# The mixing of a hybrid trunk layer: projections in small groups, gates and decays through DRAM, heads as series of steps in an order set by a rule

## The chip, the cores and the metric

The kernel runs on one core of one Trainium2 chip. The metric is the device time of one execution in microseconds (us); lower is better. Three executions of the kernel before took 2176.93, 2179.14 and 2181.32 us, with the median at 2179.14.

## What is computed

One layer of a diffusion trunk over 1024 latent tokens, preceded by 256 context tokens that run through the same weights. The model width is 1024, everything in float32. A layer is a half-step SwiGLU feed-forward network, a token mixing and a second half-step network:

```python
x = x + 0.5 * m_l[2][:, None, :] * swiglu(modulate(rms_norm(x, ...), ...), ffn1_w1[i], ffn1_w3[i], ffn1_w2[i])
ctx = ctx + 0.5 * m_c[2][:, None, :] * swiglu(...)
y_l, y_c = token_mixing(modulate(rms_norm(x, ...), ...), modulate(rms_norm(ctx, ...), ...), w_in[i], ...)
x = x + m_l[5][:, None, :] * y_l
x = x + 0.5 * m_l[8][:, None, :] * swiglu(...)
return rms_norm(x, final_norm_w)
```

The mixing projects the tokens with one weight `w_in` and runs two groups of heads, each forwards and backwards: four heads of retention (keys of 128, chunks of 128 tokens, rotary positions, a fixed decay for each head), and four of gated linear attention (GLA; keys of 64, chunks of 64, a decay for each key and token). The latent scans start from the context's final states.

```python
# retention, one chunk
scores = jnp.einsum('bhid,bhjd->bhij', qc, kc) * decay
o = jnp.einsum('bhij,bhje->bhie', scores, vc) + jnp.einsum('bhid,bhde->bhie', qc * q_dec, s)
s = chunk_dec * s + jnp.einsum('bhjd,bhje->bhde', kc * k_dec, vc)
# GLA gates: log decays from a rank-16 projection
g_f = split_heads(jax.nn.log_sigmoid((p[8] @ w_f + b_f).astype(jnp.float32)), GLA_HEADS) / GLA_TAU
# at the end each head is normalised, scaled, multiplied with a silu gate and projected
return jnp.concatenate([r, gl], axis=-1).astype(dtype) @ w_out
```

## The kernel before

**Number format.** A large product is made of three TensorE products of split numbers: `split` (lines 60 and 61) makes a high part on ScalarE and the rest on VectorE or GpSimd, and `mm3` (lines 65 to 67) issues high x high, low x high and high x low into one accumulator. The small products of the heads (128 x 128) are plain float32, two passes each.

**Stages.** First network, context network and context projections (up to about 916 us), then the mixing of the latent tokens (`lat_phase`), the output projection (`mixed_out`) and the second network. In all but the mixing TensorE runs long rows of large products. The latent tokens go in two groups of 512 (`tg` 0 and 1).

**The mixing.** `lat_phase` (line 1309) runs a list of calls, `SEQ`: projections of a pair of GLA heads, gates, context heads, projections of retention heads, head by head. Projections: `gla_proj_pair` (values and the input `p89T` of the gates with `proj_v`, then queries and keys), `ret_proj` (queries and keys with the rotary turn: a copy with partitions exchanged by SP's queue, lines 1101 to 1108), `gate_proj` (silu gates `sg`). Their results stay in SBUF (`qk`, `vt`, `sg`). `proj_v` copies out four accumulators `psa` (lines 919 and 922); the 32-column copies `p` (922) are transposed (923) into `p89T`. There are four accumulators `psa` for projections, and others, `psb`, for the heads.

**Heads.** `gla_gates` (line 1112) makes the gate tiles of one head and group: a product (1118), the softplus on ScalarE (812 to 816: Abs, a load of a function table where `load` is set, Exp, Ln), a subtraction on VectorE, seven sums on GpSimd (1126) and two Exps (1128, 1129). `gla_mix` makes scores on seven block sizes: copies into `zq` and `zk` (1156 to 1159), a product (1163), a multiplication of A on VectorE (1183) and B on GpSimd (1184); the two largest sizes use small products (1174, 1175). Then come key transposes (1199), state updates (1205, 1212) and output products (1219, 1220). `ret_mix` has key transposes (1252), products for states (1265), scores (1278) and output (1291, 1293), statistics (1297, 1299), a power on GpSimd (`pow_half`, 1072 and 1073) and the normalisation (1305). Both end in `finish` (1054): four transposes on TensorE (1059), a multiplication with norm weight and silu gate (1066), and a store to `mixd` in DRAM by SP's queue. Where the silu gate isn't made yet, retention heads 2 and 3, the tile is kept (1062) and multiplied in `mixed_in` (1351).

**What sets the order.** A scheduler puts every engine's instructions in order from the program order, priorities and its own times. `high_priority(offset=-...)` with `FPRI`, `VPRI`, `RPRI` and `CRP` moves transposes of `finish`, state products, key transposes and context products back; weight loads have an own priority. A queue runs in its order, so an instruction that waits holds up what stands behind it. SP's queue issues loads; GpSimd's issues the stores of the networks (`self.store`, line 351) and none in the mixing.

## Time and profile before

| | before |
|---|---|
| runs, median (lowest to highest) | 2179.14 us (2176.93 to 2181.32) |
| profiled execution: time, span of the trace | 2177.08 us, 2175.3 us |
| TensorE busy | 2115.8 us, 97% |
| VectorE, ScalarE, GpSimd busy | 1533.8, 980.5, 367.3 us |
| mean granted clock of TensorE, of full speed | 0.995 |

The rows below come from one profiled execution, whose time differs a little from its span, since what lies before the first and after the last instruction is not in the span. PE is TensorE, DVE VectorE, ACT ScalarE, POOL GpSimd; L12 is line 12 of the kernel. The time of a matmul record includes its filling of the array, so records overlap and the pitch from start to start is shorter.

### The profile page before, as it was taken

Reading aid. Unit: us, or ns where it says so; the run is one execution under the profiler, and the core shown is the slowest. Engines: PE = TensorE matmul, PEld = TensorE weight load, DVE = VectorE, ACT = ScalarE, POOL = GpSimd, SP = SyncE. Lnnn points to the kernel's source line nnn. Section 1 sums busy time; section 2 is a strip of 40 time slices with the busy share of each in tenths; the row PEclk is TensorE's granted clock in tenths of the full one; section 3 lists DMA queues with packets and bytes.
Section 4 is the critical chain, followed back from the end, with each engine's and each line's share of the span. In section 5 each row is a group of like instructions: output and inputs, shape, how many; then the busy total and the mean of one; then the engine's idle time right before and its main releaser. Section 6 shows DMA issues by size and latency. Waiting matters only on the chain. (4 is left out here: it accounts for less than half of the span.)

```text
span 2175.3 us, 33087 instructions
## 1 busy us (share of the span) xinstructions
PE 2115.8 (97%) x11558; PEld 1805.0 (83%) x11558; DVE 1533.8 (71%) x2747; ACT 980.5 (45%) x1811; POOL 367.3 (17%) x472
## 2 busy tenths in 40 slices
...
GB/s 331 83 232 242 266 221 270 179 241 309 296 196 172 169 184 194 184 144 104 90 65 62 103 60 82 119 92 155 63 129 161 139 155 158 155 221 242 207 242 148
DMA packets 190263, 373.40 MB, mean 172 GB/s; under 512 B 24016, under 2 KB 37264, under 8 KB 190096
## 3 DMA queue, kind: packets, MB, share of 16 engines
...
q14 instruction: 77, 0.63, 0.1%
q10 hardware_dynamic: 432, 0.13, 0.0%
...
## 5 line engine op out<-in xcount | busy, mean ns | idle before, releaser
L60 ACT ACTIVATE whi<-raw 128x512 fp32r<-128x512 f32 (+1 forms) x647 | 398.2, 622 | 667.2 <-PE psa L66 200.0
L61 DVE TENSOR_TENSOR wlo<-raw,whi 128x512 fp32r<-128x512 f32 (+1 forms) x545 | 377.4, 696 | 292.3 <-ACT whi L60 289.0
L67 PE MATMUL psa<-hh,wlo 128*128 128x512 f32 (+1 forms) x1444 | 530.0, 367 | 3.1 <-POOL wlo L61 3.1
L65 PE MATMUL psa<-hh,whi 128*128 128x512 f32 (+1 forms) x1444 | 530.6, 367 | 1.1 <-DVE s L565 0.6
L66 PE MATMUL psa<-hl,whi 128*128 128x512 f32 (+1 forms) x1444 | 529.8, 367 | 0.6 <-DVE hl L61 0.6
L67 PEld LDWEIGHTS psa<-hh,wlo 128*128 128x128 f32 x1444 | 273.3, 189 | 45.3 <-POOL wlo L61 4.1
L65 PEld LDWEIGHTS psa<-hh,whi 128*128 128x128 f32 x1444 | 273.4, 189 | 44.6 <-DVE s L565 1.0
L66 PEld LDWEIGHTS psa<-hl,whi 128*128 128x128 f32 x1444 | 273.5, 189 | 42.1 <-DVE hl L61 1.2
L65 PE MATMUL psb<-hh,whi 128*128 128x512 f32 (+1 forms) x680 | 260.0, 382 | 0.5 <-ACT whi L60 0.5
L67 PE MATMUL psb<-hh,wlo 128*128 128x512 f32 (+1 forms) x680 | 259.9, 382 | 0.6 <-DVE wlo L61 0.6
L66 PE MATMUL psb<-hl,whi 128*128 128x512 f32 (+1 forms) x680 | 259.7, 382 | 0.0
L61 POOL TENSOR_TENSOR wlo<-raw,whi 128x512 fp32r<-128x512 f32 (+1 forms) x102 | 136.7, 1358 | 204.5 <-ACT whi L60 200.5
L351 POOL DMA_DIRECT2D gd<-s x154 | 83.7, 543 | 392.1 <-DVE s L342 300.5
L67 PEld LDWEIGHTS psb<-hh,wlo 128*128 128x128 f32 x680 | 127.9, 188 | 25.7 <-DVE wlo L61 1.3
L65 PEld LDWEIGHTS psb<-hh,whi 128*128 128x128 f32 x680 | 128.0, 188 | 25.5 <-ACT whi L60 1.0
L66 PEld LDWEIGHTS psb<-hl,whi 128*128 128x128 f32 x680 | 127.9, 188 | 24.8
L66 PE MATMUL psa<-wlo,hh 128*128 128x256 f32 (+1 forms) x320 | 93.4, 292 | 1.2 <-DVE wlo L61 1.1
L65 PE MATMUL psa<-whi,hh 128*128 128x256 f32 (+1 forms) x320 | 93.3, 292 | 1.2 <-ACT s L1027 1.2
L67 PE MATMUL psa<-whi,hl 128*128 128x256 f32 (+1 forms) x320 | 92.7, 290 | 0.0
L128 DVE CUSTOM_DVE_ANT_0 junk<-ada,condc,cols 128x1024 bf16<-128x1024 f32 x62 | 79.4, 1281 | 5.7 <-DMA ada<-in_adaT 3.9
L1073 POOL TENSOR_TENSOR nr<-nr,mhalf 128x4 f32<-128x4 f32 (+1 forms) x11 | 10.6, 965 | 412.6 <-DVE nr L1072 403.0
L61 DVE TENSOR_TENSOR hl<-raw,hh 128x512 fp32r<-128x512 f32 x93 | 65.2, 709 | 10.4 <-ACT hh L60 10.3
(404 smaller groups left out, 3884.0 us busy)
## 6 DMA issues: line engine op xcount, KB each, us to landing
...
gd<-s POOLq DMA_DIRECT2D x154, 256.0 KB, 3.0
...
```

Of the source, the lines that this page charges most:

```text
L60: nc.scalar.activation(hi, src, AF.Copy)
L61: (eng or nc.vector).tensor_tensor(out=lo, in0=src, in1=hi.bitcast(F32), op=ALU.subtract)
L65: mm(ps, wa[0], xa[0], start=start, stop=False, skip_group_check=more)
L66: mm(ps, wa[0], xa[1], start=False, stop=False, skip_group_check=more)
L67: mm(ps, wa[1], xa[0], start=False, stop=stop, skip_group_check=more)
L128: nc.vector.tensor_tensor_reduce(out=self.junk, in0=t, in1=self.cs[s], scale=1.0, scalar=self.col("ada_b")[:, j:j + 1], op0=ALU.mult, op1= ...
L351: put = lambda i, t: self.store.dma_start(self.gd[i, f // 2], t)
L1073: nc.gpsimd.tensor_tensor(out=r, in0=r, in1=self.mhalf[:, :n], op=ALU.pow)
```

## The change

The arithmetic and TensorE's 10,746 products stay the same; the mixing is laid out anew.

- Projections become `units`, series of pieces of 6 or 12 products in the order of a list `UNITS`. Each unit copies its accumulators to a tile `pv` and stores it to DRAM by GpSimd's queue (`put`). Value weights are loaded once for both token groups (except those of `gv0`, which also makes the gates' input).
- Gates of all four heads of a group are made in a row (`gate_lane`), those of group 0 after the unit `ga0` and those of group 1 after `gv0`; they go to DRAM. The decays of the retention heads are made once behind the first group's gates and go to DRAM.
- Heads become four `lanes` of steps: context heads, gates, GLA heads, retention heads. A step yields the earliest time at which TensorE should take it, its cost, and the names of units and gates it needs.
- `lat_phase` writes TensorE's whole order: the step of a lane whose time has come, else the next piece of a projection. The times come from sums of VectorE's work (`vec`, times `SLACK` 1.25) and constants. The other engines are still put in order by the scheduler.
- 15 of the 16 head tiles are now multiplied with their silu gate in `mixed_in`, from DRAM, where before it were 4.
- Table loads are asked for in the first gate only. On ScalarE the program has 27 of them before and 5 after. Stores of context states and head tiles move from SP's queue to GpSimd's: 198 DMAs there before, 298 after; on SP's 1260 and 1292.

```diff
+    def finish(self, on, tg, wcol, hb, pool):
         nc = self.nc
         pt = self.psB()
-        with self.tc.high_priority(offset=-FPRI):
-            for c in range(4):
-                nc.tensor.transpose(pt[:, c * P:(c + 1) * P], on[:, c * P:(c + 1) * P], self.ident)
-        if sg is None:
-            t = self.tile(pool, [P, 512], F32, "qk", 8)
-            nc.scalar.activation(t, pt, AF.Copy, scale=wcol)
-            self.late[hb, tg] = t
+        for c in range(4):
+            nc.tensor.transpose(pt[:, c * P:(c + 1) * P], on[:, c * P:(c + 1) * P], self.ident)
+        mx = self.t2(pool)
+        if hb in self.gated:
+            sg = self.tile(pool, [P, 512], F32, "sg", 2)
+            nc.sync.dma_start(sg, self.sgd[hb * P:(hb + 1) * P, tg * 512:(tg + 1) * 512])
+            nc.vector.scalar_tensor_tensor(out=mx, in0=pt, scalar=wcol, in1=sg, op0=ALU.mult, op1=ALU.mult)
         else:
-            mx = self.t2(pool)
-            nc.vector.scalar_tensor_tensor(out=mx, in0=pt, scalar=wcol, in1=sg[tg], op0=ALU.mult, op1=ALU.mult)
-            nc.sync.dma_start(self.mixd[hb * P:(hb + 1) * P, tg * 512:(tg + 1) * 512], mx)
+            self.late.add((hb, tg))
+            nc.scalar.activation(mx, pt, AF.Copy, scale=wcol)
+        self.store.dma_start(self.mixd[hb * P:(hb + 1) * P, tg * 512:(tg + 1) * 512], mx)
...
+    def gate_lane(self, pool):
+        nc = self.nc
         for tg in LATTG:
...
+            yield 0, 0, (("ga0", "gv0")[tg],)
+            for h in range(4):
+                yield self.now, 0.45, ()
+                self.gla_gates(h, tg, pool)
+                self.done[f"G{tg}{h}"] = self.vec(1.4) + 6
+            if tg == 0:
+                for h in range(4):
+                    self.decays(h, pool)
+
+    def decays(self, h, pool):
+        nc = self.nc
+        tab = lambda i: self.tab[:, i * P:(i + 1) * P]
+        dec, u = self.tile(pool, [P, 3, P], F32, "dec", 1), self.t2(pool)[:, :P]
+        lf, lb = self.lg[:, h:h + 1], self.lg[:, 4 + h:5 + h]
+        for o, i, l in ((dec[:, 0, :], 0, lf), (u, 1, lb), (dec[:, 1, :], 2, lf), (dec[:, 2, :], 3, lb)):
+            nc.scalar.activation(o, tab(i), AF.Exp, scale=l)
+        nc.vector.tensor_tensor(out=dec[:, 0, :], in0=dec[:, 0, :], in1=tab(4), op=ALU.mult)
+        nc.vector.tensor_tensor(out=u, in0=u, in1=tab(5), op=ALU.mult)
+        nc.vector.tensor_tensor(out=dec[:, 0, :], in0=dec[:, 0, :], in1=u, op=ALU.add)
+        self.store.dma_start(self.decd[h], dec.rearrange("p i t -> p (i t)"))
+        self.done[f"D{h}"] = self.vec(0.6) + 4
...
-        self.softplus(a, zp, bias, tg in LXG)
+        self.softplus(a, zp, bias, (h, tg) == (0, 0))
...
+        self.store.dma_start(self.ggd[h, tg], g)
+        self.store.dma_start(self.gLd[h, tg][:, :508], L[:, :508])
+
+    def vec(self, us):
+        self.dve = max(self.dve, self.now) + SLACK * us
+        return self.dve
...
+            ons.append((self.vec(1) + 3 - 2 * (tg == 0), on))
+        for tg in LATTG:
+            yield ons[tg][0], 0.9, ()
+            self.finish(ons[tg][1], tg, self.col("ret_norm_w")[:, h:h + 1], h, pool)
...
+    def put(self, pool, ps, dst, fn=AF.Copy, scale=1.0, view=None):
+        t = self.tile(pool, [P, 512], F32, "pv", 4)
+        self.nc.scalar.activation(t, ps, fn, scale=scale)
+        self.store.dma_start(dst, view(t) if view else t)
+
+    def unit(self, pool, w, dst, fn=AF.Copy, scale=1.0):
+        for tg in LATTG:
+            ps = self.psA()
+            for q in range(4):
+                yield 4 * tg + q, q // 2, 6 * 0.227
+                for k in range(2 * q, 2 * q + 2):
+                    self.mm3(ps, self.wslice(w, k), self.h[tg][k], k == 0, k == KD - 1)
+            self.put(pool, ps, dst[:, tg * 512:(tg + 1) * 512], fn, scale)
...
+    def unit_v0(self, pool, w, tg):
+        nc = self.nc
+        ps = [self.psA() for _ in range(4)]
+        for k in range(KD):
+            yield k, k, 12 * 0.133
+            for c in range(4):
+                self.mm3(ps[c][:, :288], [t[:, c * P:(c + 1) * P] for t in self.h[tg][k]], [t[:, :288] for t in w[k]], k == 0, k == KD - 1)
+        pT = self.psB()
+        if tg == 0:
+            self.pt89 = self.tile(pool, [64, 512], F32, "p89T", 1)
+        rs = []
+        for c in range(4):
+            r = self.tile(pool, [P, 32], F32, "p89", 4)
+            nc.scalar.copy(r, ps[c][:, 256:288])
+            rs.append(r)
+        t = [self.tile(pool, [P, 512], F32, "pv", 4) for _ in range(2)]
+        for c in range(4):
+            nc.scalar.copy(t[c // 2][:, c % 2 * 256:c % 2 * 256 + 256], ps[c][:, :256])
+        for c in range(2):
+            r0 = 512 * tg + 256 * c
+            self.store.dma_start(self.gvd[r0:r0 + 256, :256].rearrange("(c p) e -> p c e", p=P), t[c].rearrange("p (c e) -> p c e", c=2))
+        yield KD, None, 0.5
+        for c in range(4):
+            nc.tensor.transpose(pT[:32, c * P:(c + 1) * P], rs[c], self.ident)
+        self.p89T[tg] = self.pt89[32 * tg:32 * tg + 32]
+        nc.scalar.copy(self.p89T[tg], pT[:32])
...
+        self.now, self.dve = 0.0, 0.0
+
+        def step(lane):
+            y = next(lane[0], None)
+            if y is None:
+                lanes.remove(lane)
+            else:
+                lane[1:] = y
+
+        lanes = [[g, 0, 0, ()] for g in lanes]
+        with self.pe_order():
+            for lane in list(lanes):
+                step(lane)
+            piece = next(fill, None)
+            while lanes or piece:
+                ready = [(max([x[1]] + [done[n] + DONE for n in x[3]]), i) for i, x in enumerate(lanes) if all(n in done for n in x[3])]
+                at, i = min(ready) if ready else (1e9, None)
+                if i is not None and (at <= self.now or not piece):
+                    self.now = max(self.now, at) + lanes[i][2]
+                    step(lanes[i])
+                elif piece:
+                    name, work, pe = piece
+                    self.vec(work / SLACK)
+                    self.now += pe
+                    if name:
+                        done[name] = self.now
+                        if name[1] == "g":
+                            self.gated.add(int(name[2]) + 4 * (name[0] == "g"))
+                    piece = next(fill, None)
 
     def mixed_in(self, pool):
         nc = self.nc
...
         zt, i = [f"z{n}{h}" for h in (1, 2, 4, 8, 16) for n in "qk"], 0
         for tg in LATTG:
             for k in KORD:
+                s = (slice(k * P, (k + 1) * P), slice(tg * 512, (tg + 1) * 512))
+                raw = self.tile(pool, [P, 512], F32, zt[i % len(zt)])
+                i += 1
+                nc.sync.dma_start(raw, self.mixd[s])
                 if (k, tg) in self.late:
-                    raw = self.late[k, tg]
-                    nc.vector.tensor_tensor(out=raw, in0=raw, in1=self.late_sg[k][tg], op=ALU.mult)
-                else:
-                    raw = self.tile(pool, [P, 512], F32, zt[i % len(zt)])
-                    i += 1
-                    nc.sync.dma_start(raw, self.mixd[k * P:(k + 1) * P, tg * 512:(tg + 1) * 512])
+                    sg = self.tile(pool, [P, 512], F32, "qk", 4)
+                    nc.sync.dma_start(sg, self.sgd[s])
+                    nc.vector.tensor_tensor(out=raw, in0=raw, in1=sg, op=ALU.mult)
...
-LXC = (0, 1, 2, 3)
-LXG = (0, 1)
+LXC = (0,)
...
-SEQ = ('gla_in(0)', 'gates(0)', 'cr()', 'cg()', 'ret_in(0)', 'gla(0)', 'gates(1)', 'ret(0)', 'gla(1)', 'gates(2)', 'ret(1)', 'gla_in(1)', 'ret_in(1)', 'gla(2)', 'gates(3)', 'ret(2, False)', 'gla(3)', 'ret(3, False)')
+UNITS = ("gv0", "gk0", "gq0", "rk0", "rq0", "rv0", "rk1", "rq1", "gk1", "gq1", "gv1", "gg0", "rg0", "gg1", "rk2", "rq2", "rv1",
+         "rg1", "rk3", "rq3", "gg2", "rg2", "gg3", "rg3")
+WAHEAD, WLIVE = 3, 5
+SLACK = 1.25
+CTXAT = 16
+DONE = 6
```

Instruction orders below are rows of the two programs, in the form line, operation, out<-in, shape.

ScalarE in the start of the mixing, before: `vt` and `p` are the copies of the value projection of the second group, `p89T` the gates' input, L812 to L816 the gates of the first head.

```order
L919 COPY vt_9974<-psa_10145 128x256
L922 COPY p_2325_10300<-psa_10144 128x32
L922 COPY p_2326_10304<-psa_10145 128x32
L60 ACTIVATE whi_10759<-raw_10757 128x512
L926 COPY p89T_10123<-psb_10290 32x512
...
L812 ACTIVATE t_2348_10441<-psb_10442,cols_78 128x512
L814 ACT_TABLE_LOAD
L815 ACTIVATE t_2348_10441<-t_2348_10441 128x512
L812 ACTIVATE t_2352_10464<-psb_10465,cols_78 128x512
L816 ACTIVATE t_2348_10441<-t_2348_10441 128x512
```

After: L818, L1091 and L1092 are Ln and Exps of the gates (`sc` and `L` of heads 2 and 3), L817 their Exp, L1068 the decays, L972 a context copy, L1393 the `p` copies of the second group.

```order
L1091 ACTIVATE sc_10330<-sc_10330 128x512
L818 ACTIVATE t_2345_10345<-t_2345_10345 128x512
L1068 ACTIVATE t_2351_10379<-tab_9877,lgx_9879 128x128
L1068 ACTIVATE t_2353_10389<-tab_9877,lgx_9879 128x128
L1068 ACTIVATE t_2355_10399<-tab_9877,lgx_9879 128x128
L1092 ACTIVATE L_10320<-L_10320 128x508
L1091 ACTIVATE sc_10354<-sc_10354 128x512
L1068 ACTIVATE dec_10378<-tab_9877,lgx_9879 128x128 x3
L972 COPY t_2360_10429<-psb_10426 128x256
L1393 COPY p_2369_10485<-psa_10169 128x32
L1393 COPY p_2370_10487<-psa_10170 128x32
L1393 COPY p_2371_10489<-psa_10171 128x32
```

The `p` copies of the second group stood ahead of all gates and now stand behind the gates of four heads.

TensorE at the end of the first retention head, before: L1291 and L1293 are the head's output products, L1059 the transposes of `finish`, L65 to L67 projection products, of which 13 lie between.

```order
L1291 MATMUL psb_11716<-vt_10722,t_2574_11710 128x128
L1293 MATMUL psb_11716<-S_11646,t_2575_11712 128x128
L1293 MATMUL psb_11716<-S_11646,t_2576_11714 128x128
L65 MATMUL psa_12258<-hh_2071_9185,whi_12240 128x512
L66 MATMUL psa_12258<-hl_2072_9186,whi_12240 128x512
...
L67 MATMUL psa_12294<-hh_2061_9175,wlo_12247 128x512
L65 MATMUL psa_12294<-hh_2063_9177,whi_12246 128x512
L1059 MATMUL psb_11750<-ident_82,t_2581_11745 128x128
L1278 MATMUL psb_11758<-qk_11532,qk_11568 128x128 x4
L1059 MATMUL psb_11750<-ident_82,t_2581_11745 128x128 x3
```

After: L1342 and L1344 are output products, L1033 transposes of `finish` (the first two rows of them of a GLA head, the last of this retention head's group 0), L67 to L69 projections, of which 18 lie between.

```order
L1344 MATMUL psb_11856<-Sr_11541,t2r_11829 128x128
L1033 MATMUL psb_11893<-ident_82,t_2595_11796 128x128 x4
L1033 MATMUL psb_11901<-ident_82,t_2600_11817 128x128 x4
L67 MATMUL psa_11771<-hh_1331_5977,whi_11452 128x512
L68 MATMUL psa_11771<-hl_1332_5978,whi_11452 128x512
...
L68 MATMUL psa_11940<-hl_2068_9182,whi_11470 128x512
L69 MATMUL psa_11940<-hh_2067_9181,wlo_11471 128x512
L1342 MATMUL psb_11965<-vr_11539,t2r_11886 128x128
L1344 MATMUL psb_11965<-Sr_11541,t2r_11882 128x128
...
L1344 MATMUL psb_11965<-Sr_11541,t2r_11882 128x128
L1344 MATMUL psb_11965<-Sr_11541,t2r_11884 128x128
L1033 MATMUL psb_12006<-ident_82,t2r_11888 128x128 x4
```

The transposes of a group now come after the other head's transposes, 18 projection products and the next group's output.

GpSimd at heads' ends, before: L1184 are multiplications of the scores, L1073 the power in a head's end.

```order
L1184 TENSOR_TENSOR B_2823_13356<-B_2823_13356,L_12186 128x8x32
L1184 TENSOR_TENSOR B_2825_13362<-B_2825_13362,L_12209 128x8x32
L1184 TENSOR_TENSOR B_2823_13356<-B_2823_13356,L_12186 128x4x64
L1184 TENSOR_TENSOR B_2825_13362<-B_2825_13362,L_12209 128x4x64
L1073 TENSOR_TENSOR rr_13616<-rr_13616,mhalf_86 128x4
L1073 TENSOR_TENSOR rr_13648<-rr_13648,mhalf_86 128x4
```

After: L1048 is the power, L1145 the multiplication, L1369 and L1042 are stores of projections and head tiles.

```order
L1048 TENSOR_TENSOR rr_12620<-rr_12620,mhalf_86 128x4
L1369 DMA gvd<-pv_12779 128x2x256
L1042 DMA mixd<-t_2740_12740 128x512
L1048 TENSOR_TENSOR rr_12727<-rr_12727,mhalf_86 128x4
L1369 DMA gvd<-pv_12782 128x2x256
L1369 DMA gvd<-pv_12785 128x2x256
L1369 DMA gvd<-pv_12788 128x2x256
L1048 TENSOR_TENSOR rr_12804<-rr_12804,mhalf_86 128x4
```

Stores now stand between these instructions; ten of the 16 powers have one right ahead.

## Rows read from the trace of the kernel before

**Rows 1.** The page: busy time, share of the span and instructions of each engine

```profile
PE 2115.8 (97%) x11558; PEld 1805.0 (83%) x11558; DVE 1533.8 (71%) x2747; ACT 980.5 (45%) x1811; POOL 367.3 (17%) x472
```

**Rows 2.** Stretches: us, busy (x) of PE, PEld, DVE, ACT, POOL; clock; DMA share; GB/s

```profile
916.00:1020.00 104.00, 94.93 (x613) 84.60 (x612) 48.90 (x126) 55.11 (x130) 20.31 (x33) 0.98 0.47 134
1020.00:1440.00 420.00, 399.64 (x2736) 340.36 (x2734) 260.31 (x599) 194.17 (x373) 87.26 (x115) 1.00 0.27 81
1440.00:1462.00 22.00, 20.22 (x99) 16.50 (x100) 11.45 (x28) 7.58 (x12) 1.31 (x1) 1.00 0.32 100
```

**Rows 3.** TensorE's waits, 1020 to 1462: line, waited for, us, times, longest

```profile
PE psb L1059 <- DVE t L1305: 6.1, 5, 2.5
PE psb L1059 <- ACT t L1230: 3.7, 5, 1.0
PE psb L1163 <- ACT zq L1157: 3.2, 4, 1.0
PE psb L1174 <- POOL B L1184: 3.1, 5, 1.1
PE psb L1163 <- DVE zk L1158: 2.0, 3, 1.1
...
```

**Rows 4.** TensorE's waits, 916 to 1020, same view

```profile
PE psb L995 <- DVE t L990: 4.3, 2, 2.5
PE psb L923 <- ACT p L922: 1.4, 1, 1.4
...
```

**Rows 5.** Timeline of TensorE at the end of a lane's run

```profile
1058.08 0.48 PE L66 MATMUL psa<-hl,whi 128*128 128x512 f32 x1
1058.39 0.40 PE L67 MATMUL psa<-hh,wlo 128*128 128x512 f32 x1
1058.63 0.39 PE L65 MATMUL psa<-hh,whi 128*128 128x512 f32 x1
1058.86 0.39 PE L66 MATMUL psa<-hl,whi 128*128 128x512 f32 x1
```

**Rows 6.** Timeline of ScalarE at two gates

```profile
979.66 1.28 ACT L814 ACT_TABLE_LOAD   x1
980.95 0.63 ACT L815 ACTIVATE t<-t 128x512 f32<-128x512 f32 x1
981.49 0.67 ACT L812 ACTIVATE t<-psb,cols 128x512 f32<-128x512 f32 x1
```

**Rows 7.** Timeline of GpSimd at the first gate's sums

```profile
983.69 0.61 POOL L1126 TENSOR_TENSOR L<-sc 128x256 f32<-128x256 f32 x1 [45.11 <-DVE sc L1122]
984.39 2.43 POOL L1126 TENSOR_TENSOR L<-L 128x128 f32<-128x128 f32 x6
```

**Rows 8.** Stores of the FFN issued by GpSimd, line 351

```profile
L351 POOL DMA_DIRECT2D gd<-s x154: 539/539/736, 66.7 to 1955.7; - x154
...
DMA to landing us min/median/max: 2.2/3.0/7.3
```

**Rows 9.** Groups of VectorE by form, 925 to 1475

```profile
L1305 DVE TENSOR_SCALAR t<-psb,bmv,rr 128x128 f32<-128x128 f32 x32 | 10.9, 404 | 7.0 <-POOL rr L1073 7.0
...
L1297 DVE BATCH_NORM_STATS2 bst<-psb 128x6 f32<-128x128 f32 x32 | 7.1, 282 | 4.8 <-PE psb L1293 4.8
...
L1299 DVE BATCH_NORM_AGGREGATE bmv<-bst 128x2 f32<-128x6 f32 x32 | 2.9, 151 | 0.0
...
L1351 DVE TENSOR_TENSOR qk<-qk,sg 128x512 f32<-128x512 f32 x4 | 2.7, 686 | 0.0
...
L1072 DVE TENSOR_SCALAR rr<-bmv 128x4 f32<-128x4 f32 x8 | 1.3, 163 | 0.1
```

**Rows 10.** Groups of GpSimd by form, 925 to 1475

```profile
L1184 POOL TENSOR_TENSOR B<-B,L 128x256 f32<-128x256 f32 x48 | 40.9, 857 | 62.2 <-DVE zk L1158 45.2 <-PE psb L1175 6.4 <-DVE rr L1072 5.0
L1073 POOL TENSOR_TENSOR rr<-rr,mhalf 128x4 f32<-128x4 f32 x16 | 18.1, 1132 | 159.1 <-DVE rr L1072 159.1
```

**Rows 11.** Groups of ScalarE by form, 925 to 1475: busy us, mean ns, idle before

```profile
L1157 ACT COPY zq<-B 64x256 f32<-64x256 f32 x40 | 16.5, 411 | 47.2 <-PE psb L1163 28.6 <-POOL B L1184 14.1 <-POOL B L1155 4.3
```

484 lines of the change are left out of this document (271 added, 213 removed).

## The prediction

> **What bounds the kernel now.** I read the busy table first: TensorE is busy for 2115.8 us, 97% of the span [rows 1]. A change that leaves its matmuls alone can at most win the rest, so the question is where TensorE is not busy in the part that is rewritten, the mixing from 916 to 1462 us. The table by stretches [rows 2] gives that: in the start (916 to 1020: context heads, first gates, first projections) TensorE is busy 94.93 of 104 us, in the middle 399.64 of 420, in the last 22 us 20.22. That is 9.1 + 20.4 + 1.8 = 31.3 us, and the clock hardly enters (0.98 to 1.00). The program order has 10,746 matmuls before and after, of the same shapes; hence everything is in these 31 us and in small costs of switching.
>
> Then I read what ended TensorE's waits. From 1020 on they add up to 21.4 us in nine rows, of which the first five stand in [rows 3]: transposes at a head's end wait for VectorE's normalised tile (6.1) or ScalarE's (3.7), score products for the zq/zk copies (3.2 and 2.0), small block products for GpSimd (3.1). All are short (at most 2.5 us), 28 in number: before gives a chain too little other TensorE work to run beside. In the start, 4.3 of 8.9 us are waits of the context retention for its decayed values and 1.4 for p, the 32-column copies from which the gates' input is transposed [rows 4].
>
> **Part 1, the start: 12.6 us dearer.** After ga0 (gates' input of token group 0) TensorE issues all four heads' gate products at once, and ScalarE works them off in one row: order on ScalarE shows Abs, Exp, Ln and two more Exps for heads 0 to 2, those of head 3 but its last Exp, seven Exps of decays, and only then the p copies L1393 of the second token group. TensorE has, from the first gate product to the transposes L1403 that need these copies, the four gate products in f32 (two passes each), 48 products of 288 columns and two context transposes. By the pitch of about 0.23 us for 512 columns [rows 5], 288 columns take about 0.13, so 6.3 us for the 48, 1.8 for the gates and 0.5 for the transposes: 8.6 us. It can't go past them: the second group holds all four "psa" accumulators, which the next projection needs too.
>
> The chain on the other side, by durations of before: Abs, table load, Exp and Ln of the first head follow at a pitch of about 0.54 with the load at 1.28 [rows 6], some 3.5 us; subtraction on VectorE about 1.5; then GpSimd's seven sums of one gate, from 983.69 to 986.82, 3.1 us [rows 7], and behind them in its queue two stores at 0.54 each [rows 8]. Three gates' sums in a row, the third without its stores: 5.0 + 2 x 4.2 + 3.1 = 16.5. After the last Exp of head 2 come one of head 3, three decays and a context copy at 0.4, then the copies of 32 columns: some 20 us, and up to 23 with the hand-overs. TensorE stands 11.5 to 14.5 us; I take 13.5, nearer the upper end since weight splits stand between. To this come 2 us for the first group's copies and transposes (before 1.4), 2.7 for the second gates and a context transpose behind them, 1.5 for context loads that wait for stores, and 2 for the clock, which shows in the stretch at 0.98 even now: 21.7 us, against 9.1. Net +12.6, range +6 to +16.
>
> ScalarE loses 22 table loads of 1.28 us, 28 us of its time [rows 6]. In this chain one load remains where before each pair of gates had two. The row says that a load costs its 1.28 us and no more: load at 979.66, next Exp at 980.95. The Trainium skill (ScalarE: Activation LUTs, What ACT_TABLE_LOAD costs) adds a drain of about 1.38 us to each switch, 2.66 in all. By that rule ScalarE would get back 58 us instead of 28, and the one load that is left in the start's chain would make the time 2172.0. The trace disagrees, since nothing idles around the load, and I use neither number.
>
> **Part 2, the middle: 19 us cheaper.** The steps are now laid out so that a chain has its time beside it in projection pieces. At the end of a retention head the chain is 4 x 0.282 + 4 x 0.151 + 0.163 + 1.132 + 4 x 0.404 = 4.64 us [rows 9, 10], about 5.1 with hand-overs. Before: 13 products of 512 columns between output and transposes, 3.0 us, and TensorE waits up to 2.5 [rows 3]. After, for head 0: between the output of group 0 and its transposes lie 8 other transposes, 18 products and the output of group 1, 0.9 + 4.1 + 2.7 = 7.7 us; for group 1, 24 products and 8 small ones, 6.8. Both cover 5.1. Score products have 12 to 18 projection products ahead (2.8 to 4.1 us) instead of 6 (1.4), against copies of 0.41 us on two engines [rows 11] and one GpSimd multiplication of 0.857 [rows 10]. Of the 21.4 us of waits, with about a tenth of restart at each of 28, 24 us, I let 5 stay, since the rule counts VectorE's work and not ScalarE's, GpSimd's or the DMAs': -19, bounds -8 (16 stay) and -23 (1 stays).
>
> **Part 3, fewer returns: 3.6 us cheaper.** Where a run of small products ends, the first projection product takes 0.31 instead of 0.23 us to the next [rows 5]. In the order I count 125 such returns before and 80 after: 45 x 0.08 = 3.6 us. Bounds 0 and 5.
>
> **Part 4, traffic and the end: 1.5 us dearer.** q, k, v, gates and decays go to DRAM by about 100 more GpSimd stores, 0.539 us each to issue and 3.0 to land [rows 8]: 54 us of GpSimd, which is busy 109 of the 546 us (the three stretches of [rows 2]), and DMA engines busy 0.27. Hidden but for one place: the last retention head's transposes have 18 products ahead (4.1 us) against 5.1, and its tile then goes to DRAM and back, twice 3.0 us, and is multiplied and split. I count 9.9 us against 10.3 us of output projections that need other tiles first. The 15 late tiles instead of 4 add 11 multiplications of 0.686 on VectorE [rows 9], 7.5 us; VectorE is busy half of that last stretch. Together 1.5, bounds 0 and 6. The value weights loaded once for both groups take 12 splits off ScalarE and VectorE: nobody on the path waits for these in the middle, so nothing.
>
> **Sum** on the profiled execution (2177.08 us): 12.6 - 19 - 3.6 + 1.5 = -8.5, so 2168.6. The median of the runs lies 2.06 us higher: **2170.6 us**, 0.4% faster.
>
> **The rivals.**
> - *The start costs little.* If the copies L1393 come at the early end or GpSimd's sums do not wait for the stores (the second sums could begin 1.1 us sooner per gate), and the middle leaves 1 us: 2170.6 - 6.6 - 4 = 2160. For it: ScalarE's and GpSimd's pieces overlap at before's pitch. Against: the row on ScalarE is fixed, and four gates' sums on one engine alone are 12 us against 8.6 of cover.
> - *Slower: GpSimd's queue.* Ten of the 16 power instructions at heads' ends stand directly behind a store in GpSimd's order, often of a projection that has yet to be evicted, and none did before. A unit of projection takes 24 x 0.23 = 5.5 us; a mean wait of half, 2.8 us, is over the slack of 1.7 (6.8 less 5.1) by 1.1 us, so 11 us; the multiplications L1145 stand behind stores as well, and if the waits of the scores and blocks come back (3.2 + 3.1 + 2.0 = 8.3), the time is 2190. It decides from a mean wait of 1.7 us on. For it: the rule knows nothing of GpSimd. Against: the evictions are of units that the order has before the head's end, and waiting stores were 0.54 us each.
> - *GpSimd's stores are slow beside VectorE.* A store takes 539 ns to issue at the median and 736 at most, and lands after up to 7.3 us [rows 8], beside a busy VectorE. If all landed late: 4.3 us more at the end and 0.2 x 8 in the gates' chain, 2176.5. The Trainium skill (SBUF — State Buffer, the warning on the "DVE blocks DMA" trap) says that such a store cannot write its descriptors while VectorE runs a float32 copy in its two-port mode. The maximum of 736 beside 539 hardly shows it, though no store ran in the mixing of before, where VectorE's copies into zq and zk are.
> - *Nothing gained:* the middle keeps 14 of its waits: about 2179.
>
> **How the numbers follow.** My forecast gets 0.45, the cheap start 0.17, the slower queue 0.22, the slow stores 0.08, nothing gained 0.08. A difference under 0.2% (4.4 us) is about what a measurement of this kernel can't tell from no change, so "same" runs from 2174.8 to 2183.5. The forecast's own spread (start +6 to +16, middle -23 to -8) puts some 0.08 of its 0.45 into same. Faster: 0.37 + 0.17 + 0.01 = 0.55. Same: 0.08 + 0.07 + 0.07 + 0.01 = 0.23. Slower: 0.22. The range is 2152 to 2192: below, the cheap start at no net cost (6 us less than its +6) and the returns at their bound (1.4), 2160 - 7.4 = 2152.6; above, the queue rival at 2190 and part of the end's bound.
>
> **What would show it.** In the start of the changed trace one wait of 10 us or more at L1403 for ScalarE's p, with GpSimd's sums of three gates before it. After about 1020 us TensorE's waits sum to under 10 us, at L1033 under 3. The power instructions start within a microsecond of VectorE's input. If L1403 waits under 5 us, part 1 is wrong; if L1033 or the scores wait for GpSimd by more than before, part 2 is; and if ScalarE's busy time in the mixing does not fall by about 28 us, the table loads were miscounted.

## The result: slower by 0.4%

| | before | after |
|---|---|---|
| median of five runs | 2178.75 us | 2187.05 us |
| lowest to highest | 2176.93 to 2181.32 | 2184.12 to 2192.70 |
| ratio, 95% interval | | 1.0040, 1.0024 to 1.0057 |
| profiled execution, span | 2177.08, 2175.3 us | 2184.12, 2180.9 us |
| mean granted clock | 0.995 | 0.989 |

The changed kernel is 8.3 us slower, where 8.5 us faster was forecast. In the profiled executions the difference is 7.0 us, 5.6 us of it inside the traces' spans.

The first line of the changed kernel's page, busy time by engine:

```profile
PE 2119.4 (97%) x11558; PEld 1817.0 (83%) x11558; DVE 1529.7 (70%) x2735; ACT 948.6 (43%) x1776; POOL 420.5 (19%) x572
```

TensorE is *busy* for 3.6 us more than before [rows 1] with the same products. Some of them ran more slowly, as the clock below shows.

Stretches of the mixing, after (us of the stretch; busy time and count on PE, PEld, DVE, ACT and POOL; clock; DMA share; GB/s):

```profile
916.00:1027.00 111.00, 91.35 (x472) 74.99 (x471) 58.74 (x139) 66.63 (x154) 54.05 (x109) 0.91 0.59 192
1027.00:1440.00 413.00, 398.41 (x2844) 354.16 (x2843) 244.27 (x578) 149.15 (x308) 106.80 (x139) 0.98 0.47 147
```

The start has 111 - 91.35 = 19.65 us without TensorE, the middle 14.6, the end none. Before it was 9.1, 20.4 and 1.8 [rows 2]. Idle time in the mixing has thus grown by 3.0 us only. But the clock is 0.91 in the start and 0.98 in the middle.

TensorE's waits in the start of the changed kernel, and in the rest of the mixing (line, waited for, us, times, longest). L1403 are the transposes of the `p` copies, L950, L956, L970 and L981 steps of context heads, L1153 the scores of a GLA head and L1033 the transposes of `finish`:

```profile
PE psb L1403 <- ACT p L1393: 12.0, 2, 11.5
PE psb L981 <- ACT t L818: 3.9, 1, 3.9
PE psb L950 <- DVE t L946: 1.9, 1, 1.9
...
```

```profile
PE psb L1153 <- DVE zq L1131: 4.5, 1, 4.5
PE psb L1033 <- ACT t L1240: 3.8, 3, 2.9
PE psb L1033 <- DVE t2r L1359: 2.1, 2, 1.5
...
```

The waits of the middle that stood in [rows 3] have become fewer (12 of 14.4 us in all, against 28 of 21.4), but three of those that are left are long: 4.5, 2.9 and 1.5 us. In [rows 4] the longest was 2.5; here one is 11.5.

That one, on TensorE, then on ScalarE, then on GpSimd:

```profile
959.49 0.29 PE L69 MATMUL psa<-whi,hl 128*128 128x288 f32 x1
971.33 1.03 PE L1403 MATMUL psb<-ident,p 128*32 128x128 f32 x4 [11.54 <-ACT p L1393]
```

```profile
950.07 0.69 ACT L814 ACTIVATE t<-psb,cols 128x512 f32<-128x512 f32 x1
950.77 1.28 ACT L816 ACT_TABLE_LOAD   x1
952.07 0.63 ACT L817 ACTIVATE t<-t 128x512 f32<-128x512 f32 x1
...
957.74 0.63 ACT L1092 ACTIVATE L<-L 128x508 f32<-128x508 f32 x1 [1.72 <-POOL L L1089]
...
963.06 0.63 ACT L1092 ACTIVATE L<-L 128x508 f32<-128x508 f32 x1 [1.71 <-POOL L L1089]
...
968.87 0.63 ACT L1092 ACTIVATE L<-L 128x508 f32<-128x508 f32 x1 [1.19 <-POOL L L1089]
...
971.09 0.44 ACT L1393 COPY p<-psa 128x32 f32<-128x32 f32 x4
```

```profile
954.74 0.61 POOL L1089 TENSOR_TENSOR L<-sc 128x256 f32<-128x256 f32 x1 [3.59 <-DVE sc L1085]
955.43 2.27 POOL L1089 TENSOR_TENSOR L<-L 128x128 f32<-128x128 f32 x6
957.83 0.56 POOL L1093 DMA_DIRECT2D ggd<-sc  x1
958.77 0.54 POOL L1094 DMA_DIRECT2D gLd<-L  x1 [0.37 <-ACT L L1092]
959.70 0.98 POOL L1089 TENSOR_TENSOR L<-sc 128x256 f32<-128x256 f32 x1 [0.39 <-DVE sc L1085]
```

TensorE ends its last 288-column product at 959.8 and has its next instruction at 971.3. ScalarE goes through the gates in its fixed order: each Exp of the sums (L1092, at 957.74, 963.06 and 968.87) waits for one gate's sums on GpSimd, whose first instructions are 5.0 us apart (954.74, 959.70), the two stores L1093 and L1094 among them. The `p` copies come at 971.09, 21.0 us after the first gate's Abs at 950.07. That is the chain of the prediction, near its length.

What TensorE had to do beside it was not as counted. The prediction gave the four gate products 1.8 us, eight passes at the pitch of the large products. Before and after:

```profile
977.80 1.13 PE L1118 MATMUL psb<-p89T,wg 32*128 32x512 f32 x4
```

```profile
947.83 3.82 PE L1081 MATMUL psb<-p89T,wg 32*128 32x512 f32 x8
```

Before, the products of a head's two token groups start in pairs, within 0.01 us of each other, and the four passes take 1.1 us. After, with one group at a time, the passes follow each other at 0.43 us, and eight take 3.8. From the first of them, at 947.83, to the transposes are 23.5 us. TensorE works for 12.0 of these, not 8.6 as counted, some of it at the lower clock shown next, and stands for 11.5.

**The clock around it.** The same stretch in pieces:

```profile
946.80:951.60 4.80, 4.80 (x15) 2.06 (x13) 2.14 (x3) 2.52 (x5) 0.57 (x1) 0.97 0.92 332
951.60:954.70 3.10, 3.10 (x14) 3.08 (x14) 1.35 (x2) 3.09 (x6) 0.00 (x0) 0.50 0.40 134
...
959.80:971.30 11.50, 0.00 (x0) 0.00 (x0) 6.54 (x15) 8.26 (x22) 9.22 (x23) 0.72 0.44 154
971.30:974.80 3.50, 3.47 (x11) 2.77 (x12) 0.79 (x4) 2.67 (x10) 3.03 (x9) 0.50 0.56 230
```

From 951.3 on the granted clock was 0.50 (1.2 of 2.4 GHz) for 3.4 us, a half-clock stretch as it is called below, at the end of the four gate products, which use 32 rows; from 964.9 to 975.2 again, first while TensorE stood, then for another 3.8 us in which it worked. There are four more such stretches in the mixing, at 995.6 (6.8 us), 1132.2 (3.4), 1207.3 (3.4) and 1292.6 (6.8). Each of the four begins during a wait or at most 1.5 us behind its end; these waits are 3.9, 1.5, 2.9 and 4.5 us long. Before, there were two, of 3.4 us each, at 999.2 and 1347.3, behind waits of 2.5 and 2.0 us; a third wait of 2.5 us, at 1117.3, had none. The first of them, the wait and the stretch behind it:

```profile
995.20:997.60 2.40, 0.00 (x0) 0.03 (x1) 1.96 (x7) 2.33 (x7) 1.05 (x2) 1.00 0.43 104
998.80:1002.20 3.40, 3.40 (x19) 3.38 (x19) 2.69 (x8) 1.67 (x4) 0.68 (x1) 0.55 0.35 117
```

**The account.** I counted, from TensorE's records and the granted clock of windows of 0.4 us, for each kernel the time from the first 288-column product to a fixed product of the second network (the 2780th from the end of the three-product kind), the idle time in it, and half of the time that TensorE worked at half clock. What is left is work at full clock:

| kernel | stretch | idle | lost by the clock | rest |
|---|---|---|---|---|
| before | 655.9 | 34.2 | 3.4 | 618.3 |
| after | 662.3 | 36.4 | 12.8 | 613.1 |

So the order did make the work itself 5.2 us cheaper; the idle time grew by 2.2 in this longer stretch, and the clock took 9.4 us more. The sum, +6.4, is the difference of the stretches. The rest of the span adds -0.8 us.

### The profile page after: what moved, and what is told of

Read it like the earlier page. It is cut to its first block, busy times and chain, and to the rows that moved or that the text cites. A ratio compares the mean times of both kernels' runs of the same rounds, so it can differ in the third digit from the quotient of the medians.

```text
span 2180.9 us, 33346 instructions
## 1 busy us (share of the span) xinstructions
PE 2119.4 (97%) x11558; PEld 1817.0 (83%) x11558; DVE 1529.7 (70%) x2735; ACT 948.6 (43%) x1776; POOL 420.5 (19%) x572
## 4 chain that ended last, share of the span: by engine, by line
PE 79%; DVE 6%; issue 5%; DMA 4%; POOL 2%; ACT 2%; SPq 0%; POOLq 0%; ACTq 0%; DVEq 0%
PE psa L67 14%; PE psa L69 14%; PE psa L68 14%; PE psb L67 10%; PE psb L69 9%; PE psb L68 9%; PE psa L1421 3%; PE psb L1153 2%; DVE hl L226 1%; POOL L L1089 1%; DVE nt L220 1%; DMA qk<-sgd 1%; DMA raw<-in_w 1%; PE psb L1301 1%; POOL rr L1048 0%
## 5 line engine op out<-in xcount | busy, mean ns | idle before, releaser
L62 ACT ACTIVATE whi<-raw 128x512 fp32r<-128x512 f32 (+1 forms) x635 | 390.7, 622 | 673.2 <-PE psa L68 212.6
L63 DVE TENSOR_TENSOR wlo<-raw,whi 128x512 fp32r<-128x512 f32 (+1 forms) x533 | 368.2, 694 | 251.6 <-ACT whi L62 244.1
L67 PE MATMUL psa<-hh,whi 128*128 128x512 f32 (+1 forms) x1444 | 535.8, 371 | 2.2 <-ACT hh L62 1.1
L69 PE MATMUL psa<-hh,wlo 128*128 128x512 f32 (+1 forms) x1444 | 528.9, 366 | 3.1 <-POOL wlo L63 3.1
L67 PEld LDWEIGHTS psa<-hh,whi 128*128 128x128 f32 x1444 | 275.4, 191 | 47.1 <-ACT hh L62 1.9
L69 PEld LDWEIGHTS psa<-hh,wlo 128*128 128x128 f32 x1444 | 274.2, 190 | 48.0 <-POOL wlo L63 4.1
L67 PE MATMUL psb<-hh,whi 128*128 128x512 f32 (+1 forms) x680 | 259.6, 382 | 0.5 <-ACT whi L62 0.5
L69 PE MATMUL psb<-hh,wlo 128*128 128x512 f32 (+1 forms) x680 | 259.5, 382 | 0.6 <-DVE wlo L63 0.6
L69 PEld LDWEIGHTS psb<-hh,wlo 128*128 128x128 f32 x680 | 127.8, 188 | 25.7 <-DVE wlo L63 1.0
L67 PEld LDWEIGHTS psb<-hh,whi 128*128 128x128 f32 x680 | 127.8, 188 | 25.5 <-ACT whi L62 1.0
L1048 POOL TENSOR_TENSOR nr<-nr,mhalf 128x4 f32<-128x4 f32 (+1 forms) x11 | 10.3, 932 | 423.1 <-DVE nr L1047 413.5
L385 POOL DMA_DIRECT2D sd<-s x22 | 11.9, 541 | 359.3 <-DVE s L384 359.2
L62 ACT ACTIVATE hh<-raw 128x512 fp32r<-128x512 f32 x93 | 57.0, 620 | 12.2 <-DMA raw<-gd 9.8
L352 DVE TENSOR_TENSOR s<-s,s 128x512 f32<-128x512 f32 x88 | 59.0, 685 | 0.4
```

The lines of the kernel that those rows point to most:

```text
L62: nc.scalar.activation(hi, src, AF.Copy)
L63: (eng or nc.vector).tensor_tensor(out=lo, in0=src, in1=hi.bitcast(F32), op=ALU.subtract)
L67: mm(ps, wa[0], xa[0], start=start, stop=False, skip_group_check=more)
L69: mm(ps, wa[1], xa[0], start=False, stop=stop, skip_group_check=more)
L352: sub = lambda o, a, b: nc.vector.tensor_tensor(out=o, in0=a, in1=b, op=ALU.subtract)
```

## Experiments

All but the two probes start from the changed kernel. Times are medians; ratios are against the kernel before, run in turn on the same chip (there 2179.53, 2178.01 and 2176.92 us in the three groups). The changed kernel was not run again beside them, so differences to its 2187.05 us are good to 2 or 3 us. The last column is the account as above, for the profiled execution of each run:

| run | time | ratio, 95% interval | stretch = idle + clock + rest |
|---|---|---|---|
| e8_prio | 2186.88 | 1.0037 (1.0023 to 1.0051) | 668.0 = 38.7 + 15.6 + 613.7 |
| e5_spread | 2179.76 | 1.0001 (0.9989 to 1.0012) | 652.9 = 30.6 + 7.4 + 614.9 |
| e2_filler | 2188.06 | 1.0048 (1.0030 to 1.0065) | 668.1 = 27.7 + 16.7 + 623.7 |
| e3_rope2 | 2190.22 | 1.0046 (1.0031 to 1.0062) | 666.5 = 37.4 + 17.2 + 611.9 |
| f1_spread_ctx | 2183.37 | 1.0023 (1.0013 to 1.0032) | 659.2 = 34.9 + 11.0 + 613.3 |
| f3_room | 2173.85 | 0.9979 (0.9969 to 0.9989) | 650.0 = 27.4 + 10.8 + 611.8 |
| e4_loads_back | 2193.55 | 1.0075 (1.0058 to 1.0092) | 670.3 = 45.4 + 11.3 + 613.6 |
| e7_sp_stores | 2179.79 | 1.0013 (1.0002 to 1.0023) | 657.8 = 34.9 + 9.5 + 613.4 |
| b_pause0 | 2186.87 | 1.0050 (1.0033 to 1.0066) | 664.8 = 38.5 + 8.1 + 618.2 |
| b_pause16 | 2197.67 | 1.0095 (1.0078 to 1.0111) | 676.4 = 49.3 + 8.9 + 618.2 |
| g1_room_sp | 2165.29 | 0.9941 (0.9923 to 0.9958) | 641.5 = 23.5 + 4.9 + 613.1 |
| g3_all | 2164.16 | 0.9940 (0.9920 to 0.9959) | 643.7 = 25.9 + 6.0 + 611.8 |

The rest is 618.3 for the old order, 612 to 615 for the new one (e2_filler has 10.9 us of added work in its 623.7), whatever was done to the waits.

Single runs of one kernel differ by 5 us and more here (the kernel before from 2172 to 2183 us in 29 runs), which is as much as one or two half-clock stretches; a profiled execution may lie some us off its kernel's median.

### The `p` copies ahead, by priority alone

```diff
-            nc.scalar.copy(r, ps[c][:, 256:288])
+            with self.tc.high_priority(offset=3000):
+                nc.scalar.copy(r, ps[c][:, 256:288])
```

> Changed kernel with one thing more: the 32-column p copies on ScalarE get a priority, so that those of the second token group stand behind the first head's gates instead of behind all four; TensorE's order is the changed kernel's. Theory A (the loss is the 11.5 us wait at L1403 and the lower granted clock behind long waits): the wait falls under 3 us, the half-clock stretch at 964.8 to 974.8 goes, and the time falls by 11 to 15 us, to some 2172 to 2176. Rival B (the gates' chain itself is the limit; a later step waits instead): waits at L981, L950 or the first scores grow by what L1403 loses, and the time stays at 2183 to 2188.

The time did not change (2186.88). The waits of this run:

```profile
PE psa L67 <- ACT pv L1398: 7.4, 1, 7.4
...
PE psb L1404 <- ACT p L1394: 5.1, 3, 2.5
```

The wait at the transposes (L1404 here) fell from 12.0 to 5.1 us, but the next instruction, a product, then waited 7.4 us for `pv`: it needs an accumulator, and the copies that free it were still behind the gates. Rival B, at another place than it named: two waits stood behind the same queue, and only one had been lifted.

### Gates five microseconds apart

```diff
-                yield self.now, 0.45, ()
+                yield self.now + (5 if h else 0), 0.45, ()
```

> Changed kernel, but a head's gate product comes 5 us of projection work after the one before instead of at once. Theory A: no wait at L1403 over 2 us, waits at L981 and L950 under 2 us as ScalarE and GpSimd are not behind, no half-clock stretch before 1000 us; time 2168 to 2174. It also has no row of four 32-row gate products, so the half-clock stretch at 951 goes if that row brought it. Rival B (the GLA heads start later and that time is missing at the end): idle time shows up at the end of the mixing, time 2180 to 2187.

2179.76 us, 7.3 less than the changed kernel and level with the kernel before. The wait at L1403 is 1.7 us at most, the half-clock stretches at 951 and 965 are gone. The time is outside theory A's range and at the lower edge of rival B's, as there are two waits that were not there, each with its half-clock stretch (10.2 us from 995.5, 6.8 from 1026.3):

```profile
PE psb L950 <- DVE t L946: 6.8, 2, 5.8
PE psb L1153 <- ACT zq L1132: 4.3, 1, 4.3
...
```

Idle time at the end of the mixing, rival B's sign, did not appear: TensorE is busy for all of 1440 to 1462. So spreading the gates gives back 7.3 of the 8.3 us, net of the new waits, by the wait and the clock that theory A named; its size was too hopeful.

### Work in the place of the wait

```diff
+        if tg == 1:
+            yield KD, None, 0.0
+            for i in range(48):
+                nc.tensor.matmul(pT, self.h[tg][i % KD][0][:, :P], self.h[tg][i % KD][0], start=True, stop=True)
```

> Changed kernel with 48 products of 512 columns, whose result is not used, put ahead of the transposes L1403 of the second group: TensorE works through what was the 11.5 us wait. Theory A (the granted clock falls because TensorE stood): the clock is 1.00 between 962 and 975, the wait is under 1.5 us, and the kernel is 1 to 3 us faster than the changed one though it does 11 us more work: 2184 to 2186. Rival C (the clock falls there for another reason than the wait): the half-clock stretch remains and the time is the same or, with the products at half speed, up to 11 us longer.

2188.06 us. The stretches from 957 on:

```profile
957.00:974.00 17.00, 17.00 (x90) 14.73 (x90) 9.49 (x19) 12.04 (x31) 12.76 (x30) 0.98 0.50 168
974.00:984.00 10.00, 8.96 (x32) 5.49 (x30) 2.29 (x7) 6.03 (x15) 3.98 (x9) 1.00 0.65 228
984.00:992.00 8.00, 5.10 (x14) 4.13 (x15) 2.08 (x4) 3.48 (x7) 5.62 (x15) 0.57 0.53 188
```

TensorE works through what was the wait, the wait at the transposes is 0.4 us, and the clock is full from 957.7 to 985.0: the half-clock stretch of that place came from standing, and rival C falls there. But the 10.9 us of work gained nothing, and the time is not the 2184 to 2186 of theory A: TensorE now waits longer for a context head's load (3.9 us at 983) and at L950 (4.9 us), each with a half-clock stretch of 6.8 us. The chains behind the start are late in any case, and if TensorE doesn't wait at the one it waits at the next.

### Two buffers for the rope tables

```diff
-            rope = self.tile(pool, [P, 2, 512], F32, "rope", 1)
+            rope = self.tile(pool, [P, 2, 512], F32, "rope", 2)
```

Its reason is the wait of 4.5 us at 1288.9 in the changed kernel. VectorE there:

```profile
1291.63 0.69 DVE L1265 TENSOR_TENSOR qk<-rq,rope 128x512 f32<-128x512 f32 x1 [4.68 <-DMA rope<-in_rope]
...
1292.95 0.28 DVE L1131 COPY zq<-A 64x256 f32<-64x256 f32 x1
```

VectorE idles 4.68 us for the load of a rope table that a retention head needs, and behind that in its queue stands the copy L1131 for a GLA head, for which TensorE waits. The other wait, of 2.9 us at 1204, is on GpSimd: VectorE's input of the power L1048 is there at 1202.5, the power starts at 1205.0, behind two multiplications of the next GLA head, L1129 and L1145, the second of which waits 0.52 us for a gate tile that the new layout fetches from DRAM:

```profile
1202.39 1.29 POOL L1129 TENSOR_TENSOR B<-B,sc 64x512 f32<-64x512 f32 x1 [2.50 <-issue]
1204.20 0.84 POOL L1145 TENSOR_TENSOR B<-B,sc 128x256 f32<-128x256 f32 x1 [0.52 <-DMA sc<-ggd]
1205.01 1.46 POOL L1048 TENSOR_TENSOR rr<-rr,mhalf 128x4 f32<-128x4 f32 x1
```

> Changed kernel with two buffers for the rope tables instead of one (and all 16 head tiles multiplied late, which makes the room). Theory D (VectorE's rope product stands at the head of its queue for a rope load that waits for its buffer, and the GLA head's zq copy stands behind it): the waits of 4.5 us at L1153 (1289) and 1.5 us at L1033 (1129) and the half-clock stretches behind them go; 6 us of waits and 4.6 us of clock, time 2176 to 2179. Rival E (the load comes late since SP's queue is in order): the waits stay, time 2185 to 2188.

2190.22 us. Theory D named the cause: the wait at 1289 is gone, and so is the one of 1.5 us. Its gain did not come, though, and the time is in neither range: idle time is 37.4 us (36.4 in the changed kernel) and the clock takes 17.2 (12.8). A wait of 2.1 us at 1437.7 has a half-clock stretch of 6.8 us behind it, and the same pair of lanes met 150 us earlier on the next single buffer, `rs`, with a wait of 3.6 us at L1153:

```profile
1136.92 0.69 DVE L1266 TENSOR_TENSOR rs<-rs,rope 128x512 f32<-128x512 f32 x1 [1.83 <-DMA rs<-rkd]
```

### More room in the rule

Twice with the gates five microseconds apart; first at two places, then at a third:

```diff
-        yield self.vec(3) + 5, 0.44, ()
+        yield self.vec(3) + 12, 0.44, ()
...
-        yield self.now + 4, 0, ()
+        yield self.now + 9, 0, ()
```

> The kernel with the gates 5 us apart, and with more room in the rule's constants at two places: the context GLA transposes L950 come 12 us after their gate's chain instead of 5, the first scores of a GLA head 9 us after its loads instead of 4. Theory A (time is a constant of 613 us for the mixing plus idle time plus what the half clock costs behind the waits): the waits at L950 (6.8 us) and the first L1153 (4.3) go, with the half-clock stretches at 995 (10.2) and 1026 (6.8), so 8 us of waits and 5 of clock less than the spread kernel: 2167 to 2172, faster than the kernel before by 0.3 to 0.5%. Rival B (steps only move, something waits later instead): 2177 to 2181.

2183.37 us, above the ranges of both theories and slower than with the gates apart alone. L950 waits no more, but the next context step L956 waits twice (10.2 us), and scores once for 5.5 us:

```profile
PE psb L956 <- ACT t L952: 10.2, 2, 5.9
...
PE psb L1153 <- DVE zq L1131: 5.5, 1, 5.5
...
```

```diff
-            return self.vec(w) + 0.9
+            return self.vec(w) + 1.4
```

> As the run before, and the rule lets half a microsecond more pass between the zq and zk copies and the scores (1.4 instead of 0.9). Theory A: the remaining waits of the scores shrink by 1 to 3 us more, 2165 to 2171. Rival B: no more than the run before, 2168 to 2181, since the lanes get longer and end without projections beside them.

2173.85 us: faster than both kernels, 0.21% under the one before, though 2.9 us above theory A's range. Of the waits these are the longest:

```profile
PE psb L1033 <- ACT t L1240: 10.1, 6, 3.5
PE psb L956 <- ACT t L952: 4.3, 1, 4.3
...
```

Half a microsecond in one constant made 9.5 us between these two runs. The account says how: 7.5 us less idle time, and the clock alike. Which waits meet which queue depends on the whole order; that a constant is right at one place could not be read from that place.

### The table loads back

```diff
-LXC = (0,)
+LXC = (0, 1, 2, 3)
...
-        self.softplus(a, zp, bias, (h, tg) == (0, 0))
+        self.softplus(a, zp, bias, True)
```

> Changed kernel with the table loads asked for in every gate again, latent and context, as before the change (the tables stay as they are where no load is needed). The theory of the prediction: ScalarE's time is not the limit but for the chain to L1403 and L981, where two or three more loads of 1.28 us stand; waits there grow by 2.5 to 4 us, 2189 to 2193. Rival (loads are hidden): 2185 to 2189, no change.

2193.55 us, 6.5 more and 0.6 above the theory's range. Ten more loads run in the mixing, and the waits of the start grow:

```profile
PE psb L1403 <- ACT p L1393: 14.9, 2, 14.4
PE psb L981 <- DVE t L976: 8.8, 1, 8.8
...
```

The wait at L1403 is 14.4 us instead of 11.5, and the one at L981 8.8 instead of 3.9. On ScalarE three more loads stand ahead of the `p` copies, 3.8 us by their duration of 1.28, of which 2.9 reach TensorE; ScalarE's waits for GpSimd in this chain shrank by 0.6 us, and the rest isn't followed up. So the loads were not hidden, as the theory had it. The Trainium skill (ScalarE: Activation LUTs, What ACT_TABLE_LOAD costs) has 2.66 us for a switch to a different set of tables, 1.28 of it the load and 1.38 a drain. These three ask again for the set that is already there, so they don't test that figure, and the prediction's 58 us took such loads for switches too. But in the changed kernel's timeline above the Exp follows the load of 950.77 at 952.07, with no drain between. Without TensorE the start has 26.8 us instead of 19.65, the middle 15.3 instead of 14.6: fewer loads are a gain of the change, nearly all of it in the start.

### Stores by SP's queue

```diff
+        self.store = self.nc.sync
         self.masks(pool)
...
+        self.store = self.nc.gpsimd
```

> Changed kernel with all stores of the mixing issued by SP's queue instead of GpSimd's. Rival queue of the prediction (powers and sums wait behind stores on GpSimd): the wait at L1403 shrinks by 2 to 3 us (two gates' stores of 0.54 us leave the chain), waits at L1033 by 3, and the time is 2179 to 2184. Theory A: powers wait for work of the other lane more than for stores, and SP's loads now stand behind stores that wait for their data, so the time is the same or longer, 2186 to 2200.

2179.79 us, 7.3 us less (5.9 by the ratios): the rival of GpSimd's queue gave the direction and the range, and my theory A did not. But it was not the chain at L1403, where the wait is 13.1 us. TensorE's longest wait behind a power, at 1204, fell from 2.9 to 0.9 us, the one at L981 from 3.9 to 2.5, and the half-clock stretches at 1132 and 1207 are gone. All 16 powers now start within 0.17 us of their input. The stores of a projection, on GpSimd and on SP:

```profile
L1369 POOL DMA_DIRECT2D rkd<-pv x8: 540/581/602, 1020.9 to 1365.5; - x8
...
DMA to landing us min/median/max: 2.3/3.2/6.3
```

```profile
L1369 SPq DMA_DIRECT2D rkd<-pv x8: 319/336/425, 1021.1 to 1357.6; - x8
...
DMA to landing us min/median/max: 2.0/2.3/5.7
```

Such a store takes 0.58 us of GpSimd's queue and 0.34 of SP's, and the stores of this line land sooner (median 3.2 and 2.3 us over all shapes). Of SP's loads behind them, one of a context head made TensorE wait, for 1.2 us at L970, where it had not waited. The Trainium skill (SBUF — State Buffer, the warning on the "DVE blocks DMA" trap) would have stores on GpSimd's queue held up while VectorE runs a float32 copy in its two-port mode. The trace does not show that as a long issue (0.60 us at most for this row), and whether some of the 0.9 us of landing is of that kind no run here tells.

### The price of one wait

The kernel before with a probe in the output projection, far from the mixing; the second run has the loop, the first none. TensorE's order is the same in both.

```diff
+            with self.pe_order():
                 for m in range(KD):
...
+                    if (tg, m) == (1, 3):
+                        r = self.raw_half()[:, :P]
+                        nc.scalar.copy(r, ps[:, :P])
+                        for _ in range(16):
+                            nc.gpsimd.tensor_tensor(out=r, in0=r, in1=r, op=ALU.subtract)
+                        nc.tensor.transpose(self.psB()[:, :P], r, self.ident)
```

> The kernel before with a probe in the output projection, far from the mixing: a 128x128 copy of one accumulator is transposed by TensorE into an unused accumulator, with nothing done to it between; TensorE's order of that projection is fixed. It is the base of the pause run: 2178 to 2184 us, one wait of under 1 us at the probe, no half-clock stretch behind it.

> As the probe run, with 16 subtractions on GpSimd on the copied tile in a chain ahead of the transpose, some 7.5 us during which TensorE has to stand and no other order or work changes. Theory A (a wait is paid twice, as idle time and as a lower granted clock behind it): the clock falls to half for 7 to 10 us, part of it behind the wait, and the time is 9 to 12 us over the probe run. Rival C (the clock has other causes): 7 to 8 us over it, the length of the wait alone.

The probe alone was already a pause, so its expectation was missed: TensorE waited 5.6 us for the copy, which stood behind five other instructions in ScalarE's queue. The wait and what lies behind it, without and with the loop:

```profile
1495.70:1501.30 5.60, 0.01 (x1) 0.00 (x0) 5.60 (x9) 3.66 (x7) 0.00 (x0) 0.85 0.00 0
1501.30:1509.60 8.30, 6.59 (x15) 4.53 (x16) 5.90 (x10) 3.73 (x7) 0.00 (x0) 0.50 0.49 156
```

```profile
1498.70:1515.70 17.00, 0.05 (x1) 0.00 (x0) 12.79 (x19) 7.39 (x13) 10.12 (x16) 0.63 0.05 16
1515.70:1520.20 4.50, 4.45 (x11) 3.58 (x12) 0.00 (x0) 0.00 (x0) 0.00 (x0) 0.50 0.62 193
```

Without the loop the clock is half until 1509.6, 8.3 us beyond the wait's end. TensorE is busy for 6.59 us of these, so the clock takes 3.3; the other 1.7 are two waits for split weights. With the loop, and a wait of 17.0 us, the clock is half until 1520.2, 4.5 us beyond, which takes 2.2, and no such waits follow. By that the pause costs 5.6 + 3.3 + 1.7 = 10.6 us and 17.0 + 2.2 = 19.2.

Measured, the first is 9.95 us over the kernel before (2186.87 against 2176.92). That is not the pause alone, as the fixed order moved other things too: a wait of 2.3 us stands at 1374.6 where there was one of 1.1, and a half-clock stretch at 1486.0, ahead of the probe. The second is 10.8 us more than the first, where 8.6 follows. This lies in theory A's 9 to 12, but not by its mechanism: the loop took 10.1 us instead of 7.5, the wait grew by 11.4, more than the time, and the clock's share did not grow. A wait of 5.6 us thus cost some ten with what came behind it, a third of it by the clock; a long wait pays for the clock once, as a short one does.

### Room and SP's stores together

The diff is that of f3_room and that of e7_sp_stores.

> The best kernel so far (gates 5 us apart, more room in the rule at three places) with all stores of the mixing issued by SP's queue instead of GpSimd's. If the two gains add (the stores' 7 us and the room's 13): waits at L1033 for t of L1240, 10.1 us, fall under 5, and the time is 2166 to 2171. If the spread gates had already taken what the stores cost: 2172 to 2176.

2165.29 us, 0.59% under the kernel before (0.42 to 0.77%) and 1.0% under the changed one. Stretches as above:

```profile
916.00:1027.00 111.00, 103.38 (x569) 84.66 (x568) 63.81 (x154) 74.06 (x170) 35.50 (x75) 0.98 0.67 213
1027.00:1440.00 413.00, 399.17 (x2851) 355.63 (x2850) 254.15 (x587) 150.41 (x309) 66.32 (x74) 0.99 0.48 153
```

7.6 us without TensorE in the start and 13.8 in the middle, at a clock of 0.98 and 0.99. The gains add, to 0.7 us less than the range for that, though the waits at L1033 for t of L1240 fell to 7.8 us and not under 5. The middle's idle time is nearly that of the changed kernel, but none of its waits is over 2.7 us, and three half-clock stretches of 3.4 us are left of six with 34 us.

```diff
-        yield self.now + 2, 0.44, ()
+        yield self.now + 6, 0.44, ()
...
-            ons.append((self.vec(0.8) + 4.5, on))
+            ons.append((self.vec(0.8) + 6, on))
```

> As the run before, with 1.5 us more in the rule ahead of the GLA heads' last transposes and 4 us more between the two context GLA steps. Theory A: waits at L956 (4.3 us) and L1033 go with their half-clock stretches (6.8 and 6.8), 2162 to 2169. Rival B: the lanes end later and their tail stands bare, no faster than the run before.

2164.16 us, no different from the run before (intervals 0.9923 to 0.9958 and 0.9920 to 0.9959), as rival B had it; theory A's range holds the time too. L956 waits no more and L1033 for 2.4 us in all, but TensorE now waits 7.0 us at L1153 for VectorE's cT and 3.6 at L1301, each with a half-clock stretch of 6.8 us begun in it.

## Where the prediction failed

Two steps of the sum failed, of like size: the clock, which took 7.4 us more than its term, and the waits that stay in the middle, of which 5.8 us went where 16.4 were to go.

**Part 1, the start.** The mechanism held, the wait behind ScalarE's row of gates. Taken without the 2 us for the clock the sum said 19.7 us of idle time, and 19.65 were measured; that it fits so well is luck. The wait at L1403, taken at 13.5, is 11.5, the low end of its range: the chain from the first gate product was 23.5 us (20 to 23 said) and the work beside it 12.0 (8.6 said), two errors that cancel. The other terms were 0.5 us instead of 2 for the first copies, 5.8 at L981 and L950 instead of 2.7, nothing for the loads instead of 1.5, and 1.9 that no term had. ScalarE's busy time in the mixing fell by 33 us (256.9 to 223.5 in the three stretches), so the table loads were not miscounted. e5_spread shows that the bunch of gates is what the kernel lost.

**The clock: the first step that failed.** "The clock hardly enters" was read from a mean of 0.98 to 1.00 over a hundred and more microseconds, and in the sum it stood at 2 us, for the start alone. It cost 12.8 us instead of 3.4, 9.4 more, of the 12.8 about half in the start (951 to 1002) and half behind three waits of the middle. The trace of before had the evidence: of its three waits of 2.0 to 2.5 us two had a half-clock stretch of 3.4 us behind them. I had the price of a wait as its length.

**Part 2, the middle: the second.** The covers worked out for the retention heads' ends did cover, and score products no longer wait in most heads. Still 14.6 us of idle time stayed from 1027 on where I had 5 us of waits: 5.8 us less than before, not 16.4, and with the end 7.6. The longest of what stayed is not a chain that was too long for its cover, but one lane held up by another on a shared queue: VectorE by a rope load (4.5 us), GpSimd's power by multiplications (2.9). The other 7 us were not followed one by one. I had put "the rule counts VectorE's work and not the others'" at 5 us, and it was three times that. And since before's waits were short (most about 1 us), only two of them had a half-clock stretch behind them; the few that came instead are longer, and most do. Saving idle time in short waits and getting it back in long ones is a loss.

**Part 3, fewer returns.** 3.6 us for the returns and 2.8 for the restarts inside part 2 were 6.4 together; the rest of the account fell by 5.2. Near, but in part by luck: the gate products, which the change takes from four rows of 1.06 us to two of 3.75 and 3.62, became 3.1 us dearer, and the prediction had nothing for that; the other work fell by some 8.3. No run here tests the returns by themselves.

**Part 4.** The end: no idle time from 1440 to 1462, so -1.8 instead of +1.5. The stores were taken as hidden. e7_sp_stores says that on GpSimd's queue they cost 6 to 7 us in the changed kernel, with waits in the middle and their clock among it, of which part 2's excess and the clock's contain a share.

**The sum** in idle time, clock and work: predicted -8.5; measured in the profiled execution +6.4 for the stretch: start +10.6 (as predicted), middle and end -7.6 and work -5.2 (predicted together -21), the clock +9.4 (predicted +2); the start's agreement is the luck told above. The rest, -0.8, is idle time between the mixing and the end of the stretch.

**The rivals.** The slower one gave 2190, near 2187, but by its mechanism only in part. The powers waited 0.33 us on average behind VectorE's input, not 2.8, and over 1.1 us only once; what held that one, for 2.5 us, were multiplications. That GpSimd's queue with its stores costs time was right, and I had given it 0.22. "Nothing gained" kept 14 us of the middle's waits, near the 14.4 that stayed, and had 0.08. The range, 2152 to 2192, held the time; the chance of slower was too small for a sum of a large loss and a large gain, of which the loss could be read instruction by instruction and the gain only by analogy.

**What stays open.** Why the clock fell at 951.3, at the end of the gate products, without any wait. Six kernels have the same two rows of four gate products, and in each a half-clock stretch begins in one of these rows or within 2.1 us behind it: at the first row in the changed kernel, e2_filler and e3_rope2 (there with a wait of 0.9 us in it), at the second in e8_prio, e7_sp_stores and, behind a wait of 1.4 us, e4_loads_back. In the five kernels with the gates apart none does. That points to the row, but these kernels differ in more, and no run tests it alone. Open is also which part of the stores' 6 to 7 us is GpSimd's time and which is landing.
